# Two small helper products of a two-layer transformer kernel replaced: the relative distances' row written by GpSimd, the forget gate's partial sums added by ScalarE and VectorE

## The chip, the cores and the metric

The kernel runs on one core of a Trainium2 chip. The metric is the device time of one execution in microseconds (us), as the median of the runs shown. The core's engines are TensorE (PE in the profile, with its weight loads listed as PEld), VectorE (DVE), ScalarE (ACT), GpSimd (POOL) and SyncE (SP), which here only issues transfers. Each engine works through its own instructions in order and waits for the others by semaphores.

## The reference

A decoder trunk of two layers over 256 tokens with 1024 features, all in float32. Layer 0 mixes tokens by attention with a forget gate, layer 1 by attention with a learned bias on the relative distance (its block choice has no effect at this length, since 256 tokens are a single block). Each layer then has a feed-forward network (2816 wide) and a gated per-layer input.

```
for i in (0, 1):
    u = rmsnorm(h, attn_norm_g[i])
    if i == 0:                                   # forgetting attention, 16 heads of 64
        q, k, v, f_logit = split(u @ fox_w_in)   # f_logit: one column for each head
        log_f = log_sigmoid(f_logit + fox_b_f)
        c = cumsum(log_f over tokens)
        logits = q k^T / 8 + c[t] - c[s]         # causal
    else:                                        # relative bias from a table, 32 buckets x 16 heads
        q, k, v = split(u @ moba_w_in)
        logits = q k^T / 8 + rel_bias_table[bucket(t - s)]   # causal
    h += softmax(logits) v @ w_o[i]
    g, w = split(rmsnorm(h, ffn_norm_g[i]) @ ffn_w_in[i])
    h += (silu(g) * w) @ ffn_w_out[i]
    h += sigmoid(rmsnorm(h, ple_norm_g[i]) @ ple_w_gate[i]) * (p[i] @ ple_w_up[i])
return rmsnorm(h, final_norm_g)
```

`bucket` maps distances 0 to 15 to buckets of their own and larger ones to 16 buckets of growing width, the last of which holds everything from the 113th distance on.

## The kernel before, in words

The activations stay in SBUF for the whole run, features on partitions: `hx` holds 8 blocks of 128 features by 256 tokens. The weights are read once from DRAM as 216 tiles of 128 x 1024 numbers, in the order in which they are used, by SyncE's queue into a ring of six buffers (`raw`). Each is split in two for TensorE's faster float format: ScalarE copies it rounded into `whi`, VectorE subtracts that from `raw` into `wlo` (`half`, L188 and L189; `blocks` by way of L164 and L169). Each product is then three matmuls, high x high, high x low and low x high (`mm3`, L98 to L100), added in a PSUM bank. In what follows, tile k is the k-th weight tile.

The program is written as one sequence; a scheduler places the instructions on the engines' queues by its own estimate of when their inputs are ready, so that an edit moves neighbouring instructions too. `attention(0, ...)` begins with the value projection: for each of 8 feature blocks k it multiplies tokens by tile k into four banks `v` (the first three by L467, the others by `tokens`, L98 to L100). Between these stand a few helper steps:

- `nm.root()` and `nm.spread()` make the first norm's factors. The squares' sums `ss` are added over partitions by matmuls into `pr` (L250); VectorE turns them into the mean square `ms` (L251); GpSimd raises it to the power -0.5, `col` (L253); ScalarE and VectorE make the diagonal matrices `dg` from it, high and low part, two halves each (L257, L259); two matmuls by a matrix of ones spread them over all partitions into `pr` (L295), from where they are copied to `row`.
- `fox_bias` (called as `mid` in block k = 5) makes the forget gate. The gate's 16 weight columns `wf32`, padded to 32, are multiplied with `hx` in four column groups of TensorE at once (L376), so that the bank `pf` holds four partial sums on partitions 0, 32, 64 and 96. Before the change these are split into two parts (`fparts`) and added by a product with a 0/1 matrix `pick` (`total`, L386). `rest` then multiplies by the norm's row, adds the bias, takes the logarithm of the sigmoid, sums over tokens, and spreads the result through DRAM (`cd`) into `bias`, to which GpSimd adds the causal mask 32 times (L408, L409).
- `distances` makes `rv`, a row of 384 numbers for each head: the negated table entry of the bucket of each distance 255 to 0, and 1e30 beyond. Before the change it is a product of the table, split in two (`rr`), with a 0/1 matrix `ht` of buckets by distances (L425), and one VectorE instruction that negates it and adds the 1e30 from `rm` (L426). `moba_bias` stores it to DRAM (`d1`, L431, a transfer on SyncE's queue) and later spreads it for layer 1 (`d2`).

Small constants come in one transfer, `cs` from `cst` (L318): the identity, the causal mask, `pick`, the gate's weights, the table `rl` and the gate's bias. The matrix `hot` and the row `rm` have transfers of their own (L320, L322).

Of the kernel before, what the change touches and what calls it, by code (L numbers as in the profile page):

```python
# [15 lines left out]
P = 128  # L16
# [18 lines left out]
GN = 64  # L35
CST = 656
EARLY = 4
# [41 lines left out]
@with_exitstack  # L79
def trunk(ctx: ExitStack, tc: tile.TileContext, pt, w, cst, gf, hot, rvm, out):  # L80
    nc = tc.nc
# [6 lines left out]
    def bank(name):  # L88
        return ps.tile([P, 512], F32, tag="bank", name=name)

    def f32(ap):
        return ap.bitcast(F32)
# [32 lines left out]

    still0 = first_line[:, 16:17].unsqueeze(2)
    nc.gpsimd.memset(first_line[:, 16:17], 0.0)
    eps = first_line[:, 24:25]
# [8 lines left out]
    cs = one.tile([P, CST], F32, name="cs")  # L137
    ident, mask, pick32 = cs[:, 0:P], cs[:, P:2 * P], cs[:, 2 * P:3 * P]
    wf32 = cs[:, 3 * P:4 * P].rearrange("p (k h) -> p k h", h=H)
    rl, bfs = cs[0:BUCKETS, 4 * P:4 * P + H], cs[0:H, 4 * P + H:4 * P + H + 1]  # L140

# [176 lines left out]
    nc.sync.dma_start(cs, cst)  # L318
    hot32 = work.tile([BUCKETS, RVW], F32, tag="e", bufs=6, name="hot32")
    nc.sync.dma_start(hot32, hot)  # L320
    rm = work.tile([H, RVW], F32, tag="e", bufs=6, name="rm")
    nc.sync.dma_start(rm, rvm)  # L322
    ht = work.tile([P, RVW], F32R, tag="e", bufs=6, name="ht")
    nc.gpsimd.tensor_copy(ht, still0[:, 0].to_broadcast([P, RVW]))
    nc.gpsimd.tensor_copy(ht[0:BUCKETS], hot32)

    nhalf = tiny.tile([P, 2], F32, bufs=1, name="nhalf")
# [41 lines left out]
    def fox_bias(nm):  # L369
# [8 lines left out]

        pick = work.tile([P, P], F32R, tag="pt", bufs=6, name="pick")
        nc.gpsimd.tensor_copy(pick, pick32)  # L380
        parts = [work.tile([P, S], F32R, tag="pt", bufs=6, name=f"fparts{i}") for i in range(2)]
        split(*parts, pf[:, :S])

        def total():
            for i in range(2):
                mm(pf[:, S:2 * S], pick, parts[i], start=i == 0, stop=i == 1, skip_group_check=True)  # L386

        def rest():
            with tc.high_priority():
                f = work.tile([H, S], F32, tag="pt", bufs=6, name="f")  # L390
                nc.vector.tensor_tensor(f, pf[:H, S:2 * S], nm.row[:H, 1], op=ALU.mult)
                nc.vector.tensor_scalar(f, f, bfs, None, op0=ALU.add)
                a = work.tile([H, S], F32, tag="pt", bufs=6, name="fabs")
                nc.scalar.activation(a, f, AF.Abs)
                nc.scalar.activation(a, a, AF.Exp, scale=-1.0)
                nc.scalar.activation(a, a, AF.Ln, bias=1.0)
                nc.vector.scalar_tensor_tensor(f, f, 0.0, a, op0=ALU.min, op1=ALU.subtract)
                cum = work.tile([H, S], F32, tag="pt", bufs=6, name="cum")
                nc.vector.tensor_tensor_scan(cum, f, zero, 0.0, ALU.add, ALU.add)
                cd = dram.tile([H, S], F32, name="cd")  # L400
                nc.scalar.dma_start(cd, cum)
# [9 lines left out]

        return total, rest

    rv = work.tile([H, RVW], F32, tag="e", bufs=6, name="rv")

    rr = work.tile([P, 2, P], F32R, tag="pt", bufs=6, name="rr")
    nc.gpsimd.tensor_copy(rr, still0.to_broadcast([P, 2, P]))
    nc.gpsimd.tensor_copy(rr[0:BUCKETS, 0, 0:H], rl)
    nc.gpsimd.tensor_tensor(rr[0:BUCKETS, 1, 0:H], rl, f32(rr[0:BUCKETS, 0, 0:H]), op=ALU.subtract)

    def distances():

        pb = bank("pb")
        for i in range(2):
            mm(pb[:, :RVW], rr[:, i], ht, start=i == 0, stop=i == 1, skip_group_check=True)  # L425
        nc.vector.scalar_tensor_tensor(rv, pb[:H, :RVW], -1.0, rm, op0=ALU.mult, op1=ALU.add)  # L426

# [24 lines left out]
    def attention(layer, nm, mid, early, nf):  # L452
        vb = [bank(f"v{layer}_{b}") for b in range(4)]
        for c in range(4):
            wt = [early.pop(0) if early else half() for _ in range(2)]
            for kk in range(2):
# [12 lines left out]
                else:  # L469
                    for t, hf in units:  # L470
                        if layer == 0 and k == 5 and (t, hf) == units[0]:
                            total, rest = mid(nm)
                            nm.root()
                        if layer == 0 and k == 6 and (t, hf) == units[2]:
                            nm.spread(-0.125)
                            bias = rest()
                        cols = slice(hf * HC, (hf + 1) * HC)
                        tokens(vb[2 * t + hf], nm.k(k), t, (hi[:, cols], lo[:, cols]), k == 0, k == KT - 1)
# [3 lines left out]
                if layer == 0 and k == 5:  # L482
                    distances()
                    total()
            if layer == 1:
# [417 lines left out]
def _buckets():  # L903

    m = np.arange(RVW)
    n = np.maximum(S - 1 - m, 0)
    half = BUCKETS // 2
    nf = np.maximum(n, 1).astype(np.float32)
    large = half + (np.log(nf / np.float32(half)) / np.float32(math.log(MAX_DIST / half))
                    * np.float32(BUCKETS - half)).astype(np.int32)  # L910
    b = np.where(n < half, n, np.minimum(large, BUCKETS - 1))
    hot = np.zeros((BUCKETS, RVW), np.float32)
    hot[b[:S], m[:S]] = 1.0
    mask = np.zeros((H, RVW), np.float32)
    mask[:, S:] = BIG
    return hot, mask

# [66 lines left out]
```

## Time and profile before

| | us |
|---|---|
| median of 3 runs (lowest, highest) | 644.41 (643.93, 644.76) |
| span of the profiled execution | 642.4 |
| PE busy | 633.8 (99%) |
| DVE busy | 453.7 (71%) |
| ACT busy | 375.5 (58%) |
| POOL busy | 27.2 (4%) |

The profile is of one execution. Its span runs from the first to the last event on the core; no separate device time of that execution is recorded, so its own time is taken as the span plus the 2.0 us by which the median of the runs stands above it. The change lies in the first 30 us, where the page shows the transfers at 90% or more of their capacity and TensorE at its full granted clock. A row of a timeline gives the start, the duration (both us), the engine, the line, the operation, its output and inputs with their shapes, and in brackets how long the engine had been idle and what ended that. A row of the waits view gives who waited for whom, the sum in us, how often, and the longest.

### The profile page before, as it was taken

Reading aid. Unit: us, or ns where it says so; the run is one execution under the profiler, and the core shown is the slowest. Engines: PE = TensorE matmul, PEld = TensorE weight load, DVE = VectorE, ACT = ScalarE, POOL = GpSimd, SP = SyncE. Lnnn points to the kernel's source line nnn. Section 1 sums busy time; section 2 is a strip of 40 time slices with the busy share of each in tenths; the row PEclk is TensorE's granted clock in tenths of the full one; section 3 lists DMA queues with packets and bytes.
Section 4 is the critical chain, followed back from the end, with each engine's and each line's share of the span. In section 5 each row is a group of like instructions: output and inputs, shape, how many; then the busy total and the mean of one; then the engine's idle time right before and its main releaser. Section 6 shows DMA issues by size and latency. Waiting matters only on the chain.

```text
span 642.4 us, 13158 instructions
## 1 busy us (share of the span) xinstructions
PE 633.8 (99%) x5307; PEld 612.6 (95%) x5307; DVE 453.7 (71%) x781; ACT 375.5 (58%) x657; POOL 27.2 (4%) x55
## 2 busy tenths in 40 slices
PE   9999999999999999999999999999999999999995
PEld 7899999999999999999989999999999999999984
DVE  6877885786666666659896787578766666666665
ACT  8757675764444445458875586568444444454772
POOL 2118000000000000000000000000000000000002
PEclk9999999999999999999999999999999999999999
DMA  9779744376656566565687544335766666666501
GB/s 330 285 274 360 256 139 156 113 256 198 195 195 196 197 193 205 195 191 171 210 275 252 177 153 132 132 106 181 249 193 197 194 196 197 197 213 197 165 1 66
DMA packets 37020, 125.06 MB, mean 195 GB/s; under 512 B 3984, under 2 KB 6880, under 8 KB 36960
## 3 DMA queue, kind: packets, MB, share of 16 engines
q1 hardware_dynamic: 36640, 123.79, 58.3%
q8 instruction: 41, 0.67, 0.4%
q10 hardware_dynamic: 320, 0.44, 0.2%
q14 instruction: 19, 0.16, 0.1%
HBM read 123.13 MB, written 4.24 MB: 198 GB/s over the span
## 4 chain that ended last, share of the span: by engine, by line
PE 97%; DMA 1%; POOL 0%; issue 0%; ACT 0%; DVE 0%; POOLq 0%; DVEq 0%
PE gu L99 12%; PE gu L100 12%; PE gu L98 12%; PE fo L99 6%; PE fo L100 6%; PE fo L98 6%; PE pq L98 5%; PE pq L99 5%; PE pq L100 5%; PE wo L98 2%; PE wo L99 2%; PE wo L100 2%; PE pg L99 2%; PE pg L98 2%; PE pg L100 2%; PE v L98 2%
## 5 line engine op out<-in xcount | busy, mean ns | idle before, releaser
L189 DVE TENSOR_TENSOR wlo<-raw,whi 128x1024 fp32r<-128x1024 f32 (+1 forms) x198 | 237.6, 1205 | 110.5 <-ACT whi L188 105.1
L188 ACT ACTIVATE whi<-raw 128x1024 fp32r<-128x1024 f32 (+1 forms) x198 | 205.4, 1041 | 151.0 <-PE gu L99 56.3
L99 PE MATMUL gu<-g,whi 128*128 128x256 f32 x702 | 193.8, 276 | 0.0
L98 PE MATMUL gu<-g,whi 128*128 128x256 f32 x702 | 193.8, 276 | 0.0
L100 PE MATMUL gu<-g,wlo 128*128 128x256 f32 x702 | 193.8, 276 | 0.0
L100 PEld LDWEIGHTS gu<-g,wlo 128*128 128x128 f32 x702 | 131.8, 188 | 0.0
L98 PEld LDWEIGHTS gu<-g,whi 128*128 128x128 f32 x702 | 131.8, 188 | 0.0
L99 PEld LDWEIGHTS gu<-g,whi 128*128 128x128 f32 x702 | 131.8, 188 | 0.0
L98 PE MATMUL fo<-fh,whi 128*128 128x256 f32 x352 | 97.3, 276 | 0.0
L100 PE MATMUL fo<-fh,wlo 128*128 128x256 f32 x352 | 97.2, 276 | 0.0
L99 PE MATMUL fo<-fl,whi 128*128 128x256 f32 x352 | 97.2, 276 | 0.0
L98 PE MATMUL pq<-g,whi 128*128 128x256 f32 x256 | 71.1, 278 | 0.0
L100 PE MATMUL pq<-g,wlo 128*128 128x256 f32 x256 | 70.8, 276 | 0.0
L99 PE MATMUL pq<-g,whi 128*128 128x256 f32 x256 | 70.7, 276 | 0.0
L98 PEld LDWEIGHTS fo<-fh,whi 128*128 128x128 f32 x352 | 66.1, 188 | 0.0
L99 PEld LDWEIGHTS fo<-fl,whi 128*128 128x128 f32 x352 | 66.1, 188 | 0.0
L100 PEld LDWEIGHTS fo<-fh,wlo 128*128 128x128 f32 x352 | 66.1, 188 | 0.0
L98 PEld LDWEIGHTS pq<-g,whi 128*128 128x128 f32 x256 | 48.1, 188 | 1.1 <-issue 0.7
L99 PEld LDWEIGHTS pq<-g,whi 128*128 128x128 f32 x256 | 48.1, 188 | 0.1
L100 PEld LDWEIGHTS pq<-g,wlo 128*128 128x128 f32 x256 | 48.1, 188 | 0.0
L337 ACT ACTIVATE fh<-sg 128x256 fp32r<-128x256 f32 x44 | 18.1, 415 | 49.5 <-DVE sg L647 49.5
L164 ACT ACTIVATE whi<-raw 128x256 fp32r<-128x256 f32 (+3 forms) x44 | 25.5, 623 | 25.2 <-PE pq L99 8.3
(186 smaller groups left out, 983.9 us busy)
## 6 DMA issues: line engine op xcount, KB each, us to landing
raw<-w SPq DMA_DIRECT2D x212, 512.0 KB, 3.6
d<-d SPq DMA_DIRECT2D x4, 768.0 KB, 10.7
raw<-w SPq DMA_DIRECT2D x8, 256.0 KB, 4.4
bias<-d SPq DMA_DIRECT2D x4, 512.0 KB, 7.0
bias<-cd SPq DMA_DIRECT2D x2, 768.0 KB, 6.6
gx<-w SPq DMA_DIRECT2D x1, 512.0 KB, 5.3
bias<-cd SPq DMA_DIRECT2D x1, 512.0 KB, 4.3
p<-pt SPq DMA_DIRECT2D x2, 256.0 KB, 3.8
```

What stands on the lines that cost most here:

```text
L98: mm(o, ah, bh, start=start, stop=False, skip_group_check=True)
L99: mm(o, ah, bl, start=False, stop=False, skip_group_check=True)
L100: mm(o, al, bh, start=False, stop=stop, skip_group_check=True)
L164: nc.scalar.activation(o, raw[:, c], AF.Copy)
L188: nc.scalar.activation(hi[:, c], raw[:, c], AF.Copy)
L189: nc.vector.tensor_tensor(lo[:, c], raw[:, c], f32(hi[:, c]), op=ALU.subtract)
L337: nc.scalar.activation(hi, src, AF.Copy)
```

## The change

`distances` no longer multiplies. The table comes transposed and with its buckets in descending order in `cs` (`near`, one row for each head). GpSimd first fills `rv` with 1e30, early in the program. Distances of one bucket are neighbours in `rv`, so that the row falls into 32 runs, of 143, 14, 12, 10, 10, 8, 7, 6, 6, 5, 4, 4, 3, 3, 2, 3 and sixteen times 1 column; GpSimd writes each of the first 16 by one instruction that reads a single table column for all columns of the run and multiplies by -1, and the last 16 by one more. `fox_bias` no longer multiplies by `pick`: ScalarE copies the second, third and fourth partial sum out of PSUM onto partitions 0 to 15, and VectorE adds the first and the three copies. The operands `rr`, `ht`, `pick`, `hot` and `rm` with their GpSimd instructions and two transfers go, and `cst` shrinks from 656 to 448 columns.

```diff
-    ident, mask, pick32 = cs[:, 0:P], cs[:, P:2 * P], cs[:, 2 * P:3 * P]
-    wf32 = cs[:, 3 * P:4 * P].rearrange("p (k h) -> p k h", h=H)
-    rl, bfs = cs[0:BUCKETS, 4 * P:4 * P + H], cs[0:H, 4 * P + H:4 * P + H + 1]
+    ident, mask = cs[:, 0:P], cs[:, P:2 * P]
+    wf32 = cs[:, 2 * P:3 * P].rearrange("p (k h) -> p k h", h=H)
+    near, bfs = cs[0:H, 3 * P:3 * P + BUCKETS], cs[0:H, 3 * P + BUCKETS:3 * P + BUCKETS + 1]
...
     nc.sync.dma_start(cs, cst)
-    hot32 = work.tile([BUCKETS, RVW], F32, tag="e", bufs=6, name="hot32")
-    nc.sync.dma_start(hot32, hot)
-    rm = work.tile([H, RVW], F32, tag="e", bufs=6, name="rm")
-    nc.sync.dma_start(rm, rvm)
-    ht = work.tile([P, RVW], F32R, tag="e", bufs=6, name="ht")
-    nc.gpsimd.tensor_copy(ht, still0[:, 0].to_broadcast([P, RVW]))
-    nc.gpsimd.tensor_copy(ht[0:BUCKETS], hot32)
...
-        pick = work.tile([P, P], F32R, tag="pt", bufs=6, name="pick")
-        nc.gpsimd.tensor_copy(pick, pick32)
-        parts = [work.tile([P, S], F32R, tag="pt", bufs=6, name=f"fparts{i}") for i in range(2)]
-        split(*parts, pf[:, :S])
-
-        def total():
-            for i in range(2):
-                mm(pf[:, S:2 * S], pick, parts[i], start=i == 0, stop=i == 1, skip_group_check=True)
+        parts = [work.tile([H, S], F32, tag="pt", bufs=6, name=f"fparts{g}") for g in range(1, groups)]
+        for g in range(1, groups):
+            nc.scalar.activation(parts[g - 1], pf[GC * g:GC * g + H, :S], AF.Copy)
+        for g, q in enumerate(parts):
+            nc.vector.tensor_tensor(parts[0], pf[:H, :S] if g == 0 else parts[0], q, op=ALU.add)
...
-                nc.vector.tensor_tensor(f, pf[:H, S:2 * S], nm.row[:H, 1], op=ALU.mult)
+                nc.vector.tensor_tensor(f, parts[0], nm.row[:H, 1], op=ALU.mult)
...
-    rr = work.tile([P, 2, P], F32R, tag="pt", bufs=6, name="rr")
-    nc.gpsimd.tensor_copy(rr, still0.to_broadcast([P, 2, P]))
-    nc.gpsimd.tensor_copy(rr[0:BUCKETS, 0, 0:H], rl)
-    nc.gpsimd.tensor_tensor(rr[0:BUCKETS, 1, 0:H], rl, f32(rr[0:BUCKETS, 0, 0:H]), op=ALU.subtract)
+    nc.gpsimd.memset(rv, BIG)
 
     def distances():
 
-        pb = bank("pb")
-        for i in range(2):
-            mm(pb[:, :RVW], rr[:, i], ht, start=i == 0, stop=i == 1, skip_group_check=True)
-        nc.vector.scalar_tensor_tensor(rv, pb[:H, :RVW], -1.0, rm, op0=ALU.mult, op1=ALU.add)
+        runs = _runs()
+        one_each = sum(m1 - m0 == 1 for m0, m1 in runs)
+        for i, (m0, m1) in enumerate(runs[:len(runs) - one_each]):
+            nc.gpsimd.tensor_scalar(rv[:, m0:m1], near[:, i:i + 1].to_broadcast([H, m1 - m0]), -1.0, None, op0=ALU.mult)
+        nc.gpsimd.tensor_scalar(rv[:, S - one_each:S], near[:, BUCKETS - one_each:BUCKETS], -1.0, None, op0=ALU.mult)
...
                 if layer == 0 and k == 5:
                     distances()
-                    total()
...
+def _runs():
+
+    b = _buckets()
+    edges = [0] + [m for m in range(1, S) if b[m] != b[m - 1]] + [S]
+    assert len(edges) == BUCKETS + 1 and b[0] == BUCKETS - 1
+    return list(zip(edges, edges[1:]))
```

The edit also moves instructions in the engines' orders, at three places on which the prediction rests. A name's number tells buffers apart and differs between the two programs.

GpSimd, from the first instruction that needs `cs` to the root `col`. Before:

```order
L418 CAST rr<-cs 32x16
L380 CAST pick<-cs 128x128
L419 ISA
L419 TENSOR_TENSOR rr<-cs,rr 32x16
L325 CAST ht<-hot_153 32x384
L253 TENSOR_TENSOR col_277<-ms_273,nhalf 128x2
```

And now (the runs between the third and the last are left out):

```order
L410 ISA
L410 TENSOR_SCALAR rv<-cs 16x143
L410 TENSOR_SCALAR rv<-cs 16x14
...
L410 TENSOR_SCALAR rv<-cs 16x3
L411 TENSOR_SCALAR rv<-cs 16x16
L251 TENSOR_TENSOR col_269<-ms_265,nhalf 128x2
```

Four instructions between `cs` and `col` became seventeen.

VectorE, from the second sum of squares (`ss`) to the second half of `dg`. Before, `wlo` are the low parts of tiles 5, 6, 7 and the first quarter of tile 8:

```order
L234 TENSOR_TENSOR ss_225<-ss_225,sq_6_233 128x512
L236 TENSOR_TENSOR ss_225<-ss_225 128x256
L189 TENSOR_TENSOR wlo_239<-raw_237,whi_238 128x1024
L251 TENSOR_SCALAR ms_273<-pr_272 128x2
L189 TENSOR_TENSOR wlo_304<-raw_302,whi_303 128x1024
L338 TENSOR_TENSOR fparts_269<-pf,fparts_268 128x256
L189 TENSOR_TENSOR wlo_310<-raw_308,whi_309 128x1024
L169 TENSOR_TENSOR wlo_405<-raw_403,whi_404 128x256
L259 SCALAR_TENSOR_TENSOR dg_279<-cs,col_277,dg_279 128x128 x2
```

And now, the `wlo` being of tiles 5, 6 and 7:

```order
L232 TENSOR_TENSOR ss_214<-ss_214,sq_6_222 128x512
L187 TENSOR_TENSOR wlo_228<-raw_226,whi_227 128x1024
L234 TENSOR_TENSOR ss_214<-ss_214 128x256
L187 TENSOR_TENSOR wlo_307<-raw_305,whi_306 128x1024
L249 TENSOR_SCALAR ms_265<-pr_264 128x2
L373 TENSOR_TENSOR fparts_255<-pf,fparts_255 16x256
L373 TENSOR_TENSOR fparts_255<-fparts_255,fparts_256 16x256
L373 TENSOR_TENSOR fparts_255<-fparts_255,fparts_257 16x256
L257 SCALAR_TENSOR_TENSOR dg_271<-cs,col_269,dg_271 128x128
L187 TENSOR_TENSOR wlo_313<-raw_311,whi_312 128x1024
L257 SCALAR_TENSOR_TENSOR dg_271<-cs,col_269,dg_271 128x128
```

Tiles 5 and 6 moved ahead of the fold of `ss` and of `ms`, and tile 7 moved between the two halves of `dg`, which is now closer to the front.

SyncE's queue, from the constants on; `raw` are tiles 5 and up. Before:

```order
L318 DMA cs<-cst 128x656
L320 DMA hot_153<-hot 32x384
L322 DMA rm<-rvm 16x384
L185 DMA raw_237<-w 128x1024
L185 DMA raw_302<-w 128x1024
L185 DMA raw_308<-w 128x1024
L155 DMA raw_403<-w 128x1024
L185 DMA raw_435<-w 128x1024
L185 DMA raw_468<-w 128x1024
L185 DMA raw_498<-w 128x1024
L431 DMA d_391<-rv 16x384
```

And now:

```order
L316 DMA cs<-cst 128x448
L183 DMA raw_226<-w 128x1024
L183 DMA raw_305<-w 128x1024
L183 DMA raw_311<-w 128x1024
L416 DMA d_394<-rv 16x384
L153 DMA raw_406<-w 128x1024
```

The store of `rv` moved ahead of the loads of tiles 8 to 11.

More of the change, by code (lines that the diff above doesn't have):

```diff
@@ L35 @@
 GN = 64
-CST = 656
+CST = 448
 EARLY = 4
@@ L79, in trunk @@
 @with_exitstack
-def trunk(ctx: ExitStack, tc: tile.TileContext, pt, w, cst, gf, hot, rvm, out):
+def trunk(ctx: ExitStack, tc: tile.TileContext, pt, w, cst, gf, out):
     nc = tc.nc
@@ L124, in trunk @@
     table(AF.Square)
-    still0 = first_line[:, 16:17].unsqueeze(2)
-    nc.gpsimd.memset(first_line[:, 16:17], 0.0)
     eps = first_line[:, 24:25]
@@ L410, in rest @@
             return lambda i: (first[:, i], c[:, i])
-        return total, rest
+        return rest
     rv = work.tile([H, RVW], F32, tag="e", bufs=6, name="rv")
-    rr = work.tile([P, 2, P], F32R, tag="pt", bufs=6, name="rr")
-    nc.gpsimd.tensor_copy(rr, still0.to_broadcast([P, 2, P]))
-    nc.gpsimd.tensor_copy(rr[0:BUCKETS, 0, 0:H], rl)
-    nc.gpsimd.tensor_tensor(rr[0:BUCKETS, 1, 0:H], rl, f32(rr[0:BUCKETS, 0, 0:H]), op=ALU.subtract)
+    nc.gpsimd.memset(rv, BIG)
     def distances():
-        pb = bank("pb")
-        for i in range(2):
-            mm(pb[:, :RVW], rr[:, i], ht, start=i == 0, stop=i == 1, skip_group_check=True)
-        nc.vector.scalar_tensor_tensor(rv, pb[:H, :RVW], -1.0, rm, op0=ALU.mult, op1=ALU.add)
+        runs = _runs()
[3 more added lines that the diff above has]
+        nc.gpsimd.tensor_scalar(rv[:, S - one_each:S], near[:, BUCKETS - one_each:BUCKETS], -1.0, None, op0=ALU.mult)
     def moba_bias():
@@ L471, in attention @@
                         if layer == 0 and k == 5 and (t, hf) == units[0]:
-                            total, rest = mid(nm)
+                            rest = mid(nm)
                             nm.root()
@@ L903, in _buckets @@
 def _buckets():
-    m = np.arange(RVW)
-    n = np.maximum(S - 1 - m, 0)
+    n = S - 1 - np.arange(S)
     half = BUCKETS // 2
@@ L910, in _buckets @@
                     * np.float32(BUCKETS - half)).astype(np.int32)
[L911 to L916, printed above, removed]
+    return np.where(n < half, n, np.minimum(large, BUCKETS - 1))
+def _runs():
[3 more added lines that the diff above has]
+    return list(zip(edges, edges[1:]))
 def kernel(x, p, attn_norm_g, fox_w_in, fox_b_f, fox_w_o, moba_w_in, moba_w_o, rel_bias_table,
@@ L953 @@
     tri = np.where(np.arange(P)[None, :] > np.arange(P)[:, None], np.float32(BIG), np.float32(0))
-    hot, rvm = _buckets()
-    pick = (np.arange(P)[None, :] == np.arange(P)[:, None] % GC).astype(np.float32)
     cst = np.zeros((P, CST), np.float32)
-    cst[:, 0:P], cst[:, P:2 * P], cst[:, 2 * P:3 * P] = np.eye(P), tri, pick
-    cst[:, 3 * P:4 * P] = fw[:, 3 * D:].reshape(KT, P, H).transpose(1, 0, 2).reshape(P, -1)
-    cst[0:BUCKETS, 4 * P:4 * P + H], cst[0:H, 4 * P + H] = ar(rel_bias_table), ar(fox_b_f)[0]
+    cst[:, 0:P], cst[:, P:2 * P] = np.eye(P), tri
+    cst[:, 2 * P:3 * P] = fw[:, 3 * D:].reshape(KT, P, H).transpose(1, 0, 2).reshape(P, -1)
+    cst[0:H, 3 * P:3 * P + BUCKETS], cst[0:H, 3 * P + BUCKETS] = ar(rel_bias_table).T[:, ::-1], ar(fox_b_f)[0]
     xs = x[0].T.reshape(KT, P, S).transpose(1, 0, 2)
@@ L971 @@
         "gf": ar(final_norm_g)[None, :],
-        "hot": hot,
-        "rvm": rvm,
     }
```

## The prediction

> **What bounds the kernel now.** I read the page first, then the waits of TensorE (PE), then the chain of waits in order of time, and last the timelines of the other engines between 12 and 30 us. The page:
>
> ```profile
> span 642.4 us, 13158 instructions
> PE 633.8 (99%) x5307; PEld 612.6 (95%) x5307; DVE 453.7 (71%) x781; ACT 375.5 (58%) x657; POOL 27.2 (4%) x55
> ...
> PE 97%; DMA 1%; POOL 0%; issue 0%; ACT 0%; DVE 0%; POOLq 0%; DVEq 0%
> ```
>
> The reader is to see a program that is one long row of matmuls: PE makes 97% of the chain that ended last, GpSimd (POOL) almost nothing. The longest waits of PE and the only one of its matmuls show that nothing of size stands between them:
>
> ```profile
> PE cold L133 <- PEq L976: 0.8, 1, 0.8
> ...
> PEld v L467 <- ACT whi L188: 0.7, 1, 0.7
> ```
>
> So the time falls by what PE no longer does, and rises by every wait that the change puts in front of a matmul. The pieces of the chain that the change touches (start, us, what):
>
> ```profile
> 18.93 1.00 PE pf L376 x16
> ...
> 23.34 0.23 PE pf L386 x2
> ...
> 24.04 0.35 PE pb L425 x2
> ...
> 25.32 0.23 PE pr L295 x2
> ```
>
> L386 and L425 are the two helper products that go. L295 spreads the first norm's factors over the partitions from `dg`, and it keeps its place; it is where a wait can arise.
>
> **The products.** 0.23 + 0.35 us leave the chain, -0.58 us. No PE wait hides them, since PE has none there. All else that the change moves is off the chain in the kernel before, so its cost is what it makes PE wait.
>
> **The copies and adds for the forget gate.** The rows of the split and of 16x256 work of the same kind:
>
> ```profile
> 20.05 0.38 ACT L337 ACTIVATE fparts<-pf 128x256 fp32r<-128x256 f32 x1 [2.12 <-PE pf L376]
> 20.33 1.05 ACT L188 ACTIVATE whi<-raw 128x1024 fp32r<-128x1024 f32 x1
> ...
> 22.40 0.70 ACT L257 ACTIVATE dg<-cs,col 128x128 fp32r<-128x128 f32 x2 [0.72 <-POOL col L253]
> ...
> 30.70 0.40 ACT L394 ACTIVATE fabs<-f 16x256 f32<-16x256 f32 x1
> ```
>
> ```profile
> 20.50 0.16 DVE L251 TENSOR_SCALAR ms<-pr 128x2 f32<-128x2 f32 x1 [1.66 <-PE pr L250]
> 20.58 1.23 DVE L189 TENSOR_TENSOR wlo<-raw,whi 128x1024 fp32r<-128x1024 f32 x1
> 21.73 0.42 DVE L338 TENSOR_TENSOR fparts<-pf,fparts 128x256 fp32r<-128x256 f32 x1
> ...
> 23.53 0.61 DVE L259 SCALAR_TENSOR_TENSOR dg<-cs,col,dg 128x128 fp32r<-128x128 f32 x2
> ...
> 24.42 0.55 DVE L426 SCALAR_TENSOR_TENSOR rv<-pb,rm 16x384 f32<-16x384 f32 x1 [0.29 <-PE pb L425]
> ```
>
> ScalarE (ACT): three copies of 0.40 for one of 0.38, +0.8 us from 20.05. Behind them stands `whi` of weight tile 7 (the row of 20.33), which would end at about 22.2 and whose matmuls come after L295 in PE's order; `dg` waited for POOL until 22.40 anyhow. Hidden. VectorE (DVE): three adds of about 0.4 for 0.42 + 0.55, +0.25 us, in a stretch where it idled 1.66 us before 20.50; hidden too.
>
> **The transfers.** The constants shrink from 328 to 224 KB and two small loads go:
>
> ```profile
> 12.00:14.00 2.00, 2.00 (x10) 1.66 (x9) 2.00 (x5) 2.00 (x5) 0.00 (x0) 1.00 1.05 368
> ...
> cs<-cst SPq DMA_DIRECT2D x1, 328.0 KB, 6.2
> ```
>
> At 368 GB/s, 104 KB are 0.29 us: `cs` lands at about 13.8 instead of 14.09. PE does not wait for weights there, so nothing comes off the end.
>
> **The seventeen runs on GpSimd.** This is the real question. As the order in the section on the change shows, between the landing of `cs` and `col` (the first norm's root, which `dg` needs) GpSimd had four instructions. They become seventeen, and `col` stands behind all of them. Prices, from GpSimd's timeline:
>
> ```profile
> 14.09 0.31 POOL L418 CAST rr<-cs 32x16 fp32r<-32x16 f32 x1 [11.56 <-DMA cs<-cst]
> 14.35 0.28 POOL L380 CAST pick<-cs 128x128 fp32r<-128x128 f32 x1
> 14.69 1.10 POOL L419 TENSOR_TENSOR rr<-cs,rr 32x16 fp32r<-32x16 f32 x1
> ...
> 20.74 1.63 POOL L253 TENSOR_TENSOR col<-ms,nhalf 128x2 f32<-128x2 f32 x1 [4.04 <-DVE ms L251]
> ...
> 47.06 0.46 POOL L408 TENSOR_TENSOR bias<-bias,cs 128x128 f32<-128x128 f32 x1
> 47.48 1.45 POOL L409 TENSOR_TENSOR bias<-bias,cs 128x128 f32<-128x128 f32 x1
> ...
> 631.98 0.19 POOL L836 TENSOR_TENSOR colf<-ssf,msf 128x1 f32<-128x1 f32 x1 [11.94 <-ACT sqf L815]
> 632.25 0.55 POOL L846 TENSOR_TENSOR colf<-colf,nhalf 128x1 f32<-128x1 f32 x1
> 632.89 2.12 POOL L853 TENSOR_SCALAR end<-end,colf 128x512 f32<-128x512 f32 x1
> ```
>
> No row shows a TENSOR_SCALAR of 2 to 143 columns. Low end: 0.19 us (one column, nothing beside it), 17 x 0.19 = 3.2 us. Next: 0.26, from the start of the 32x16 copy to the next start, 4.4 us. High: the 512-column TENSOR_SCALAR, 2.12; as a price per column (4.1 ns x 256 columns) on top of 0.19 each it gives 4.3 us, as a fixed price it would be absurd beside 0.19. I take 0.19, the row nearest in size. Alone, the runs would thus end at 13.8 + 3.2 = 17.0 to 18.2 us, long before `col` may start at 20.74.
>
> They are not alone. Two of the rows above are far too long, 1.10 for 16 columns and 1.45 where its twin takes 0.46, and both end when a VectorE subtraction ends:
>
> ```profile
> 14.05 0.29 DVE L371 TENSOR_TENSOR fg<-cs,gx 128x128 f32<-128x128 f32 x1
> 14.31 1.40 DVE L189 TENSOR_TENSOR wlo<-raw,whi 128x1024 fp32r<-128x1024 f32 x1
> ...
> 47.07 1.54 DVE L189 TENSOR_TENSOR wlo<-raw,whi 128x1024 fp32r<-128x1024 f32 x1 [0.34 <-ACT whi L188]
> ```
>
> 14.31 + 1.40 = 15.71 against 14.69 + 1.10 = 15.79; 47.07 + 1.54 = 48.61 against 48.93. The subtraction too is longer than its usual 1.23, by about what GpSimd's earlier instruction still had to run (47.06 + 0.46 = 47.52). So each holds the other up for a whole instruction, and mostly they alternate. `col` itself is such a case: 1.63 beside the subtraction of 20.58 to 21.81, then 22.37 - 21.81 = 0.56, the 0.55 it takes undisturbed. [...]
>
> In VectorE's new order tile 6's subtraction precedes `ms` (the mean square that `col` needs), in what was idle time, but tile 7's stands between the two halves of `dg`. In strict alternation seven two-input instructions (`fg`, tile 4, two `ss` sums, tile 5, the `ss` fold, tile 6) run from 14.05 to about 20.6 and let eight runs through; nine are left, 9 x 0.19 = 1.7, and the runs end at 22.4. `col` ends 0.56 later, at 22.95. From there to L295: ACT's first half 0.40, `dg` 0.3, the subtraction 1.15 (20.58 to 21.73), `dg` 0.35, hand-overs 0.1: 2.3 us, 25.25. When PE gets there, and to two other places used below:
>
> ```profile
> 16.95 0.39 PE L99 MATMUL v<-wlo,g 128*128 128x512 f32 x1
> ...
> 25.15 0.39 PE L295 MATMUL pr<-dg,every 128*128 128x256 f32 x2
> ...
> 29.49 0.28 PE L98 MATMUL pq<-g,whi 128*128 128x256 f32 x1
> ```
>
> 25.15 - 0.58 = 24.57: PE waits 0.7 us. If two runs slip through per gap, the runs end by 21, `col` by 21.6, and PE waits nothing. I take the middle, +0.35 us, with 0 and (at 0.26 a run, ending at 23.2) 1.5 as ends.
>
> **The row's store in SyncE's queue.** Before, `d<-rv` stood behind the load of tile 11; now it stands behind tile 7, and tiles 8 to 11 wait for `rv`:
>
> ```profile
> 25.00 0.33 SPq L431 DMA_DIRECT2D d<-rv  x1
> 25.42 1.91 SPq L185 DMA_DIRECT2D raw<-w  x4
> ...
> raw<-w SPq DMA_DIRECT2D x212, 512.0 KB, 3.6
> ```
>
> With `rv` at 22.4, tile 8 is issued at 22.8, lands at 26.4 and is split by 27.5; its matmuls start at 29.49 - 0.58 = 28.9. It would bind from `rv` at 23.8 on, but by then L295 waits longer and pushes 28.9 out as far. Cost 0. Tile 12 goes out with it instead of at 25.42, so the loads catch up.
>
> **Sum.** -0.58 + 0.35 = -0.23 us. The span of the profiled execution, 642.4, becomes 642.2; the median of the runs stands 2.0 above that span, and I keep those 2.0: 644.41 - 0.23 = 644.2 us. A measurement of this kernel can tell about 0.2%, 1.3 us, from no change: 643.1 to 645.7.
>
> **Rivals.** *The runs lock VectorE out* (slower). GpSimd's copy of 14.35 ran to its end though the subtraction of 14.31 was queued: two in a row got through, so a row of short ones may keep the port. Then `fg` and tile 4's subtraction wait for all the runs, until 13.8 + 3.2 = 17.0 to 18.2, and the low part is ready 0.3 + 1.1 later, 18.4 to 19.6. PE wants it at 16.95 (tile 4's first L99), a wait of 1.5 to 2.7, net +0.9 to +2.1: 645.3 to 646.5. It decides from 0.21 us a run on. Against it: at 47.52 VectorE was let in though GpSimd's next had queued.
> *A run costs 0.4 us or more* (slower). Nine left make 3.6, the runs end at 24.2, PE waits 2.5, net +1.9: 646.3. Only the 2.12 row speaks for it.
> *GpSimd stands still before its first arithmetic instruction.* An ISA row stands ahead of the runs in the order. A hole of L us there would put the runs' end at 13.8 + L + 3.2, and the kernel would be slower than can be told from L = 6.6 on. Before, an ISA row stood ahead of L419 as well, where 0.06 us pass between 14.35 + 0.28 and 14.69, so I give it little. [...]
> *More than the products is won*, 643.0 or less. PE has no wait there to lose, and 0.58 is all it can shed; only an unseen effect, as of the later tiles' addresses, which move down by 832 bytes, could add to it.
>
> **Chances.** Forecast, with PE's wait between 0 and 1.5 us (643.8 to 645.4): 0.70. VectorE locked out: 0.14, two thirds of it beyond 645.7. Dear runs: 0.09. The hole: 0.02. More won: 0.05. Faster than 643.1: 0.05; slower than 645.7: 0.09 + 0.09 = 0.18, and 0.01 for a wait that I have not seen; the same: 0.76. The range, 643.4 to 646.4, leaves out the last rival below and the dearest ends above.
>
> **What the profile after would show.** Right: no L386 or L425 among PE's pieces; seventeen short TENSOR_SCALAR rows between 13.8 and 22.4, some stretched to over a microsecond beside `wlo`; `col` ending between 21.3 and 23.0; PE idle under 0.7 us before L293; the first `pq` matmul at 28.9 to 29.7. Wrong: PE idle before tile 4's low part near 17 us (lock-out); rows of 0.4 us with VectorE idle beside them; a hole ahead of the first run; or PE waiting for tile 8 near 29 us.

## The result: 651.1 us, 1.1% slower, and where the profile after puts it

The kernel after took 651.14 us (median of 4 runs, 650.67 to 651.69), the kernel before in the same comparison 644.32 (643.93 to 644.76): a ratio of 1.0106, 95% interval 1.0094 to 1.0118. The forecast was 644.2, with a range up to 646.4. The profiled execution took 650.67 us, so it can stand for the median; its own page reads:

```profile
span 648.9 us, 13157 instructions
...
PE 636.7 (98%) x5303; PEld 614.9 (95%) x5303; DVE 458.6 (71%) x782; ACT 376.0 (58%) x659; POOL 27.5 (4%) x66
```

PE has four matmuls less and is busy 2.9 us more, in a span that is 6.5 us longer: it both stood still and ran slower somewhere. The waits of PE name one place that the kernel before did not have, and a second behind it:

```profile
PE pq L98 <- DVE qkt L502: 3.3, 1, 3.3
PE sp L512 <- ACT pt L540: 0.9, 1, 0.9
```

**The part that the prediction looked at went as forecast.** GpSimd's timeline at the end of the runs, and PE's at the two places behind it:

```profile
21.38 0.26 POOL L411 TENSOR_SCALAR rv<-cs 16x16 f32<-16x16 f32 x1
21.61 0.72 POOL L251 TENSOR_TENSOR col<-ms,nhalf 128x2 f32<-128x2 f32 x1
```

```profile
24.54 0.45 PE L293 MATMUL pr<-dg,every 128*128 128x256 f32 x2
28.92 0.28 PE L98 MATMUL pq<-g,whi 128*128 128x256 f32 x1
```

The runs end at 21.6 and `col` at 22.3, PE reaches L293 at 24.54 without a wait, and `pq` begins at 28.92, 0.57 us earlier than the 29.49 of before. Up to here the two products are gained.

**The loss lies between 45 and 75 us.** VectorE's timeline there has one row that is unlike any other of its kind:

```profile
43.85 1.21 DVE L187 TENSOR_TENSOR wlo<-raw,whi 128x1024 fp32r<-128x1024 f32 x1
...
51.95 8.14 DVE L187 TENSOR_TENSOR wlo<-raw,whi 128x1024 fp32r<-128x1024 f32 x1 [5.79 <-ACT whi L186]
```

These are the low parts of tiles 18 and 19: the same work, 1.21 us and 8.14 us. GpSimd's timeline beside it, the 32 mask adds of L395 and L396 (first, sixteenth, seventeenth and last):

```profile
45.63 0.46 POOL L395 TENSOR_TENSOR bias<-bias,cs 128x128 f32<-128x128 f32 x1 [23.30 <-DMA bias<-cd]
...
51.88 0.46 POOL L396 TENSOR_TENSOR bias<-bias,cs 128x128 f32<-128x128 f32 x1
52.29 0.46 POOL L395 TENSOR_TENSOR bias<-bias,cs 128x128 f32<-128x128 f32 x1
...
58.55 0.47 POOL L396 TENSOR_TENSOR bias<-bias,cs 128x128 f32<-128x128 f32 x1
```

GpSimd loses nothing: one add every 0.42 us from first to last. The low part begins at 51.95, after 16 of them, and ends at 60.09, 1.07 us after the last add's end at 59.02, a little less than the 1.21 us that it takes alone. VectorE was shut out for all 16 adds that were left. In the kernel before the same subtraction, at 47.07, got in as soon as the add of 47.06 had ended. (In what follows, "the port" stands for whatever holds up an instruction of VectorE and one of GpSimd where they meet; the rows at 47.07 and 47.48 of before show such a meeting, 1.54 us for a subtraction that takes 1.21 alone and 1.45 us for an add that takes 0.46. What it is, the traces do not show.)

What hangs on it: tile 19's matmuls and `qkt` behind it on VectorE. PE's timeline:

```profile
58.44 0.28 PE L100 MATMUL pq<-g,wlo 128*128 128x256 f32 x1
62.04 0.37 PE L98 MATMUL pq<-g,whi 128*128 128x256 f32 x1 [3.33 <-DVE qkt L502]
```

And the stretches around it (start and end, length, then busy time and instructions of PE, weight loads, DVE, ACT, POOL, then the granted clock, the DMA share and GB/s):

```profile
60.00:62.00 2.00, 0.00 (x0) 0.00 (x0) 2.00 (x5) 0.00 (x0) 0.00 (x0) 1.00 0.28 70
62.00:64.00 2.00, 1.96 (x10) 1.99 (x11) 2.00 (x9) 1.86 (x8) 0.00 (x0) 0.56 0.83 268
64.00:66.00 2.00, 2.00 (x12) 2.00 (x12) 2.00 (x13) 0.75 (x4) 0.00 (x0) 0.59 0.81 209
66.00:68.00 2.00, 2.00 (x20) 2.00 (x19) 1.97 (x14) 2.00 (x10) 0.00 (x0) 1.00 0.91 333
```

After the 3.33 us of standstill PE gets 0.56 and 0.59 of its clock for 4 us and does 22 matmuls where it would do 40. That is 4 x (1 - 0.575) = 1.7 us. The wait for `pt` behind it costs more than its 0.9 us. The 16 matmuls `sp`, up to the first `po`, in the kernel before and then after:

```profile
66.63 1.58 PE L528 MATMUL sp<-qkt 64*128 64x128 f32 x16
68.14 2.17 PE L567 MATMUL po<-pt,vf 128*64 128x256 f32 x24
```

```profile
71.25 1.17 PE L512 MATMUL sp<-qkt 64*128 64x128 f32 x8
73.30 1.29 PE L512 MATMUL sp<-qkt 64*128 64x128 f32 x8 [0.89 <-ACT pt L540]
74.52 2.17 PE L551 MATMUL po<-pt,vf 128*64 128x256 f32 x24
```

They take 1.51 us before and 3.27 after, 1.76 more. Up to 58 us the matmuls start 0.57 us earlier than the same ones of before, at 74.52 `po` starts 6.38 later: 6.95 of the 7.1 us that lie between the 0.6 gained early and the 6.5 lost at the end arise here. (3.33, 1.7 and 1.76 make 6.8 of them.)

**Why the subtraction came so late.** In SyncE's queue the three `bias<-cd` loads (2 MB) stood behind tile 19 before and stand ahead of it now. The order of the two programs, between tiles 18 and 20, `-` before and `+` after, numbers left out:

```
 DMA raw18<-w 128x1024
-DMA raw19<-w 128x1024
 DMA bias0<-cd 128x1024
 DMA bias0<-cd 128x1536 x2
+DMA raw19<-w 128x1024
 DMA raw20<-w 128x1024
```

ScalarE's timelines show what it did to tile 19's high part, first before, then after:

```profile
45.98 1.07 ACT L188 ACTIVATE whi<-raw 128x1024 fp32r<-128x1024 f32 x1 [1.70 <-PE pq L99]
```

```profile
50.86 1.06 ACT L186 ACTIVATE whi<-raw 128x1024 fp32r<-128x1024 f32 x1 [7.16 <-PE pq L99]
```

It comes 4.9 us later. (The profile names PE as the releaser; DMA runs at 406 GB/s and a share of 1.01 from 46 to 50 us in the stretch view, moving the loads that went ahead.) So in the kernel after VectorE had no subtraction of this kind from 45.06 to 51.95 us, while GpSimd added and added.

That left a question that decides what to do about it: is it the late tile, the seventeen runs, or the length of GpSimd's undisturbed stream that shuts VectorE out?

### The profile page after: what moved, and what is told of

Its sections match the earlier page's. It is cut to its first block, busy times and chain, and to the rows that moved or that the text cites. A ratio compares the mean times of both kernels' runs of the same rounds, so it can differ in the third digit from the quotient of the medians.

```text
span 648.9 us, 13157 instructions
## 1 busy us (share of the span) xinstructions
PE 636.7 (98%) x5303; PEld 614.9 (95%) x5303; DVE 458.6 (71%) x782; ACT 376.0 (58%) x659; POOL 27.5 (4%) x66
## 4 chain that ended last, share of the span: by engine, by line
PE 95%; issue 2%; ACT 1%; DMA 1%; DVE 1%; POOL 0%; POOLq 0%; DVEq 0%; ACTq 0%
PE gu L98 12%; PE gu L99 12%; PE gu L100 12%; PE fo L98 6%; PE fo L99 6%; PE fo L100 6%; PE pq L98 4%; PE pq L99 4%; PE pq L100 4%; PE wo L98 2%; PE wo L99 2%; PE wo L100 2%; PE pg L98 2%; PE pg L100 2%; PE pg L99 2%; PE v L98 2%
## 5 line engine op out<-in xcount | busy, mean ns | idle before, releaser
L187 DVE TENSOR_TENSOR wlo<-raw,whi 128x1024 fp32r<-128x1024 f32 (+1 forms) x198 | 243.8, 1236 | 114.4 <-ACT whi L186 108.8
L98 PE MATMUL pq<-g,whi 128*128 128x256 f32 x256 | 72.0, 281 | 3.3 <-DVE qkt L502 3.3
L99 PE MATMUL pq<-g,whi 128*128 128x256 f32 x256 | 71.5, 279 | 0.0
L98 PEld LDWEIGHTS pq<-g,whi 128*128 128x128 f32 x256 | 48.8, 191 | 4.6 <-issue 4.2
L99 PEld LDWEIGHTS pq<-g,whi 128*128 128x128 f32 x256 | 48.8, 191 | 0.1
```

What stands on the lines that cost most here:

```text
L98: mm(o, ah, bh, start=start, stop=False, skip_group_check=True)
L99: mm(o, ah, bl, start=False, stop=False, skip_group_check=True)
L187: nc.vector.tensor_tensor(lo[:, c], raw[:, c], f32(hi[:, c]), op=ALU.subtract)
```

## Experiments

Four theories are named in the expectations. A: the late tile does it. B: the seventeen small GpSimd instructions on 16 partitions do it, so that VectorE is no longer let in at the mask adds, whenever tile 19 comes. C: chance. D, formed after the first seven runs: what counts is how many adds have run since the two engines last met on the port.

### Each half of the suspected cause by itself

**t19_first** is the kernel after with tile 19's load queued ahead of the three loads (`spreads`); the lines that collect `loads` and `spreads` are left out here:

```diff
+    def load_made(i):
+        if i == 19:
+            for d in spreads.values():
+                tc.add_manual_dep(d.ins, loads[i].ins.name, mybir.DependencyInfo(
+                    mybir.DependencyClass.NoSync, mybir.DependencyReason.DATA), reason="tile 19 first")
```

> The kernel after, with one load moved in SyncE's queue and nothing else: tile 19's weight load is issued ahead of the three bias<-cd loads, as in the kernel before, and no longer behind them. Theory A (tile 19 comes late behind the three loads, VectorE has nothing to do from 45 to 52 us, GpSimd's mask adds run on uninterrupted and then shut VectorE out until the last of them): tile 19's low part is again among the adds from their start and takes under 1.6 us instead of 8.14, TensorE does not stop at 58 us, and the time is 643.5 to 644.0, 0.6 us under the kernel before (the two products of 0.23 and 0.35 us are gone). [...]

By B a VectorE instruction of over 5 us would still be there, and the time would stay at 650 to 652.

Measured: 645.55 us, ratio 1.0039 (1.0011 to 1.0066); seven of ten executions took 644.8 to 645.7, the others 647.6, 651.6 and 652.1. VectorE in the profiled execution (645.69 us):

```profile
47.13 1.23 DVE L195 TENSOR_TENSOR wlo<-raw,whi 128x1024 fp32r<-128x1024 f32 x1 [0.34 <-ACT whi L194]
53.28 1.80 DVE L174 TENSOR_TENSOR wlo<-raw,whi 128x256 fp32r<-128x256 f32 x2 [4.93 <-ACT whi L169]
```

Tile 19 is cured, as A said, but the loads now come late, VectorE idles 4.93 us before tile 20 instead, and three of ten executions still lose some microseconds. Both theories missed the time.

**t19_last** is the kernel before with the one move that A blames, tile 19 behind the loads.

> The kernel before, both products kept, with tile 19's weight load issued behind the three bias<-cd loads, as it stands in the kernel after (the stores of d2 and two of VectorE's later splits also come a little earlier in their queues). Theory A: tile 19's low part comes only after some 6 us of mask adds, is shut out by the rest of them (6 to 9 us in place of 1.5), TensorE waits some 3 us near 60 us and then runs at a lower granted clock; the time is 650 to 652 without either part of the change. Theory B: the low part is let in after one add as before, at most 1.6 us, and the time stays within 1 us of 644.3.

Measured: 644.30 us, ratio 1.0014 (0.9995 to 1.0032): eight executions at 644.1 to 645.1, two at 648.3 and 648.6.

```profile
51.49 1.34 DVE L197 TENSOR_TENSOR wlo<-raw,whi 128x1024 fp32r<-128x1024 f32 x1 [4.70 <-ACT whi L196]
```

As late as in the kernel after, and let in. A in its plain form falls. (The two at 648 us have no trace. Their mean granted clock, 0.998 and 0.997, is that of the eight others, 0.996 to 0.998, while the profiled executions with a long low part have 0.991 to 0.995; whether they were locked stays open.)

**gate_only** and **dist_only** make one half of the change each. In both, the scheduler also puts tile 19 behind the loads.

> The kernel before with the gate's half of the change alone: ScalarE copies three quarters, VectorE adds them, the pick product of 0.23 us is gone; the distances' row still comes from TensorE's product, and no run is written by GpSimd. In SyncE's queue of this kernel tile 19's load also stands behind the three bias<-cd loads. Theory A: 650 to 652, with the long low part of tile 19. Theory B: no runs, so no lock: 644.0 to 644.3. If a third cause in the gate's part makes the time (the copies delay ScalarE's halves of tiles 13 to 15): slow here too, but without an instruction of VectorE of over 5 us near 52 us.

> The kernel before with the distances' half of the change alone: GpSimd writes the row in 17 small instructions, the product of 0.35 us with its preparation is gone; the gate's pick product stays. In SyncE's queue tile 19's load also stands behind the three bias<-cd loads. Theory A: 650 to 652, with the long low part of tile 19. Theory B: 650 to 652 as well. Were the gate's part the cause: 644.0 or less.

Measured: gate_only 644.39 us, ratio 1.0013 (0.9993 to 1.0033), with two of ten executions at 648.8 and 648.9; dist_only 652.38 us, ratio 1.0124 (1.0109 to 1.0139), all four between 651.7 and 652.9. Tile 19's low part, first gate_only, then dist_only:

```profile
50.13 1.57 DVE L189 TENSOR_TENSOR wlo<-raw,whi 128x1024 fp32r<-128x1024 f32 x1 [3.13 <-ACT whi L188]
```

```profile
53.15 8.26 DVE L188 TENSOR_TENSOR wlo<-raw,whi 128x1024 fp32r<-128x1024 f32 x1 [5.44 <-ACT whi L187]
```

The distances' half alone makes the whole loss, the gate's half none in eight executions of ten (the other two, again at a clock of 0.998 and 0.997, stay open). At this point B looked right.

### Are the runs themselves to blame?

**t19_last_runs** adds to t19_last seventeen small GpSimd writes that are overwritten afterwards:

```diff
+        at = 0
+        for i, n in enumerate(RUNS):
+            nc.gpsimd.tensor_scalar(rv[:, at:at + n], cs[0:H, i:i + 1].to_broadcast([H, n]), -1.0, None, op0=ALU.mult)
+            at += n
         pb = bank("pb")
```

> The kernel of the run t19_last (the kernel before with tile 19's load behind the three bias<-cd loads) plus 17 GpSimd instructions that write runs of 143 to 3 columns on 16 partitions of rv, ahead of L253's col as in the kernel after; the product overwrites them, so they do nothing for the result, and no other row of any engine's order differs. [...] Theory C (each execution draws anew whether VectorE is let in after some 15 adds, runs or not): as t19_last, a median near 644.3 with one or two executions in ten at 648.5.

By B tile 19's low part would take over 5 us in nearly every execution, with a median of 648 to 652.

Measured: 650.25 us, ratio 1.0079 (1.0059 to 1.0100); one of ten executions at 645.0, nine from 647.5 to 651.4.

```profile
55.59 8.10 DVE L198 TENSOR_TENSOR wlo<-raw,whi 128x1024 fp32r<-128x1024 f32 x1 [9.08 <-ACT whi L197]
```

**runs_all** is the kernel after with the runs on all 128 partitions, so that no small instruction on 16 partitions is left and every other row of the engines' orders is that of the kernel after (`near`, the runs and the store follow `rv`; those lines are left out here):

```diff
-    rv = work.tile([H, RVW], F32, tag="e", bufs=6, name="rv")
+    rv = work.tile([P, RVW], F32, tag="e", bufs=6, name="rv")
```

> [...] Theory A, sharpened (a stream that starts on a free port and runs 15 adds undisturbed locks VectorE out): still 650 to 652, with the low part of 8 us. [...]

By B the low part would be let in after one or two adds (under 1.6 us), with a median of 643.5 to 644.5, although tile 19 still comes late; by C some executions would be fast and some slow.

Measured: 647.41 us, ratio 1.0044 (1.0030 to 1.0059); five executions, 645.1, 646.0, 647.4, 647.8 and 648.0. The profiled one is the fastest of them, and there the low part is let in:

```profile
52.17 1.34 DVE L187 TENSOR_TENSOR wlo<-raw,whi 128x1024 fp32r<-128x1024 f32 x1 [5.30 <-ACT whi L186]
```

The first result fits B; the second is what C gave, with a median between those of B and A. Each of the two kernels differs from the one it starts from in one more thing, though. In t19_last_runs the runs delay `col`, with it `cum` (scanned at 38.52 us instead of 36.42) and the loads; the stream begins at 49.28 on a free port, and 16 adds run before the low part comes. In t19_last the first add, at 45.18, still met tile 18's low part, and 14 ran from there. In runs_all it was 14 again.

**port_trials** asks the port alone, without any of the kernel around it.

> No part of the reference is computed here. 36 trials one after the other: 26 GpSimd adds of 128x128 back to back, as the mask adds are; a VectorE subtraction of 128x1024, as a low part is, that comes after 1, 3 or 6 ScalarE copies of 128x1024 (some 4, 9 or 16 adds); the stream's start on a free port, or 0.3 us (B) or 0.9 us (T) into another such subtraction; and ahead of some trials 17 small GpSimd writes on 16 partitions or on 128. [...] Theory A, sharpened: it waits in the trials with a free start and 6 copies, whatever writes there were, and not in those with one copy or a blocked start. Theory C: long and short ones in each kind.

By B the subtraction would be let in ahead of the first writes on 16 partitions and behind writes on 128, and would wait for the last add behind writes on 16.

Measured, by the rows of the 36 trials: the subtraction that came after 1, 3 or 8 adds was let in within 1.33 us, 8 times of 8. After 16 adds from a free start it waited for the last one (5.4 us) 14 times of 14, and the first two of these stood ahead of any write on 16 partitions:

```profile
30.08 5.37 DVE L73 TENSOR_TENSOR wlo<-raw,whi 128x1024 fp32r<-128x1024 f32 x1 [17.35 <-ACT whi L72]
...
86.60 5.36 DVE L73 TENSOR_TENSOR wlo<-raw,whi 128x1024 fp32r<-128x1024 f32 x1 [8.19 <-ACT whi L72]
```

After a start beside another subtraction, with 16 adds begun in the one kind and 14 in the other, it waited 10 times of 14. There the first add met the other subtraction, so that 15 and 13 had run since the meeting: let in 1 time of 6 and 3 times of 8. B falls: the runs are not needed for the lock, nor do writes on 128 partitions prevent it (2 of 2 locked from a free start). What separates long from short is the number of adds, with a stretch, here at 13 and 15, in which either happens.

### How many adds shut the port

**port_curve** varies that number, and how the adds are cut.

> No part of the reference is computed here. 40 trials: 32 GpSimd adds of 128x128 back to back from a free port; a VectorE subtraction of 128x1024 comes after 1, 2, 3, 4, 5, 6 or 8 ScalarE copies of about 1.03 us (some 3, 6, 8, 11, 13, 16, 21 adds in); 26 trials so, then 7 with the same work in 16 adds of 128x256, then 7 with single adds of which the ninth has to wait some 0.2 us for ScalarE. Theory D (what decides is how many adds have run since GpSimd and VectorE last met on the port or GpSimd last waited): always let in (under 1.7 us) with up to 3 copies, nearly never with 6 and 8, a mixture at 4 and 5; with the pause after the eighth add, let in at 4 and 6 copies as well; with adds twice as wide, let in at 4 copies and likely at 6, since only half as many have run. Theory C (chance, whatever the number): short and long ones at each number alike.

From the rows, ScalarE copies ahead, adds begun, and how often the subtraction was let in within 1.7 us:

| adds of 128x128, undisturbed | 3 | 6 | 8 | 11 | 14 | 16 | 21 or 22 |
|---|---|---|---|---|---|---|---|
| copies | 1 | 2 | 3 | 4 | 5 | 6 | 8 |
| let in | 2 of 2 | 3 of 3 | 4 of 4 | 5 of 5 | 3 of 5 | 0 of 5 | 0 of 2 |

With one wait of GpSimd after the eighth add: 7 of 7 let in. The three of them that tell something came after 16, 16 and 22 adds in all, that is 8, 8 and 14 since the wait. With adds of 128x256: let in after 5, 7 and 10 adds, 6 of 6, the last of these 6.48 us after the stream's start; locked after 13 (one trial). So in these trials it is the number of instructions without a meeting or a wait that counts rather than the time: 6.48 us of single adds are 16, and 0 of 5 were let in there, against 2 of 2 after ten wide ones. Rows of VectorE's timeline: 16 adds, 11, 14 (locked), 14 (let in), ten wide ones, 16 with the wait:

```profile
17.93 7.81 DVE L65 TENSOR_TENSOR wlo<-raw,whi 128x1024 fp32r<-128x1024 f32 x1 [9.18 <-ACT whi L64]
...
49.51 1.35 DVE L65 TENSOR_TENSOR wlo<-raw,whi 128x1024 fp32r<-128x1024 f32 x1 [18.70 <-ACT whi L64]
...
117.92 8.90 DVE L65 TENSOR_TENSOR wlo<-raw,whi 128x1024 fp32r<-128x1024 f32 x1 [17.74 <-ACT whi L64]
...
185.44 1.50 DVE L65 TENSOR_TENSOR wlo<-raw,whi 128x1024 fp32r<-128x1024 f32 x1 [18.56 <-ACT whi L64]
...
470.57 1.48 DVE L65 TENSOR_TENSOR wlo<-raw,whi 128x1024 fp32r<-128x1024 f32 x1 [16.46 <-ACT whi L64]
...
574.89 1.22 DVE L65 TENSOR_TENSOR wlo<-raw,whi 128x1024 fp32r<-128x1024 f32 x1 [18.48 <-ACT whi L64]
```

With this the profiled executions of all the kernels fall into line. Adds begun since the last meeting (or since the stream's free start) when the next low part came, counted in GpSimd's timelines:

| kernel | before | in_turn (below) | gate_only | t19_first | t19_last | runs_all | dist_only | after | t19_last_runs |
|---|---|---|---|---|---|---|---|---|---|
| adds | 4 | 5 | 9 | 12 | 14 | 14 | 14 | 16 | 16 |
| low part, us | 1.54 | 1.49 | 1.57 | 0.67 (256 columns) | 1.34 | 1.34 | 8.26 | 8.14 | 8.10 |

Up to 12 all are let in, at 14 either happens, at 16 none. If executions of one kernel vary by an add or so, that would make the spread of t19_first and runs_all; only one execution of each has a trace, so that last step is argued. It would not make gate_only's two executions of 648.8 and 648.9 us, since its trace has 9.

**no_mask** takes the stream away, and with it the causal mask of the first layer, and leaves tile 19 late:

```diff
-            for i in range(H):
-                nc.gpsimd.tensor_tensor(first[:, i], c[:, i, 0:P], mask, op=ALU.add)
-                nc.gpsimd.tensor_tensor(c[:, i, P:S], c[:, i, P:S], mask, op=ALU.add)
-            return lambda i: (first[:, i], c[:, i])
+            nc.gpsimd.tensor_copy(first[:, 0, 0:1], c[:, 0, 0:1])
+            return lambda i: (c[:, i, 0:P], c[:, i])
```

> The kernel after without the 32 mask adds (GpSimd writes one column instead): the causal mask of the first layer is left out, and the order of no other engine changes. Tile 19 still comes late behind the three loads. Theories A and D: without a stream there is nothing to lock VectorE out, tile 19's low part takes 1.2 us, TensorE does not stop at 58 us, and the time is 643.4 to 644.0, 0.6 us below the kernel before. If the late tile itself, not the lock, costs the time: 646 or more.

Measured: 643.88 us, ratio 0.9996 (0.9988 to 1.0005); 0.36 us below the kernel before, not to be told from no change. The late low part is short, also in the profiled execution, the slowest of the ten (645.68 us):

```profile
53.80 1.22 DVE L187 TENSOR_TENSOR wlo<-raw,whi 128x1024 fp32r<-128x1024 f32 x1 [5.67 <-ACT whi L186]
```

The late tile costs nothing that can be measured by itself. Lock and stream together cost some 7 us (6.8 above the kernel before in the one, 0.4 below it in the other).

**in_turn** mends the cause where it arose, in SyncE's queue: bias, tile 19, bias, tile 20, bias. `ahead(a, b)` queues the load `a` ahead of `b`; `spreads` are the three loads by their first head.

```diff
+        if i == 19:
+            ahead(spreads[0], loads[19])
+            ahead(loads[19], spreads[4])
+        if i == 20:
+            ahead(spreads[4], loads[20])
+            ahead(loads[20], spreads[10])
```

> The kernel after with SyncE's queue in the order bias, tile 19, bias, tile 20, bias instead of the three bias<-cd loads in a row; no other row of any engine's order differs. VectorE's low parts of tiles 19 and 20 then come 1.5 to 4 us earlier, within some 8 adds of the last meeting, and GpSimd's later adds wait for their loads. Theory D: no low part over 2 us, 643.5 to 644.5. Theory B: locked as before, 650 to 652.

Measured: 644.90 us, ratio 1.0008 (0.9999 to 1.0016), twelve executions from 643.9 to 646.6, none near 650; the median is 0.4 above the range that theory D gave. VectorE's row, and PE's at the spread, from the slowest of the twelve:

```profile
49.41 1.49 DVE L202 TENSOR_TENSOR wlo<-raw,whi 128x1024 fp32r<-128x1024 f32 x1 [1.41 <-ACT whi L201]
```

```profile
25.47 0.39 PE L308 MATMUL pr<-dg,every 128*128 128x256 f32 x1 [0.82 <-DVE dg L272]
```

The lock is gone with every run in its old place, which is against B once more. The second row is the wait that the prediction was about: in this execution the runs ended at 22.5 us, `col` at 23.2, and PE waited 0.82.

**wide_adds** halves the number of adds: `first[:, h0:h1]` and `c[:, h0:h1, P:S]` for two heads at a time.

> The kernel after with the mask added for two heads in one instruction, 16 GpSimd adds of 128x256 in place of 32 of 128x128; same loads, same order on every other engine. Tile 19's low part then comes after 7 or 8 adds instead of 15. Theory D, if the number of instructions counts: it is let in after one add, under 2.3 us, and the time is 643.6 to 644.6. If the time of the uninterrupted stream counts rather than the number of adds: still locked until the stream's end, 650 to 652.

Measured: 650.56 us, ratio 1.0106 (1.0091 to 1.0122); four executions, 648.3, 650.0, 651.2, 652.8. Theory D missed the time here, and the median lies in the range that was expected if the time of the stream counted and not the number. In the profiled execution, the fastest, D holds for the subtraction, which came after 8 wide adds (9 with the first, which met tile 18's low part):

```profile
52.59 1.57 DVE L187 TENSOR_TENSOR wlo<-raw,whi 128x1024 fp32r<-128x1024 f32 x1 [5.04 <-ACT whi L186]
```

What costs there is another place, four microseconds of granted clock at a mean of 0.60 after a wait of PE for `pt` of 0.9 us (start and end first, the clock third from the end):

```profile
70.00:74.00 4.00, 4.00 (x28) 2.55 (x28) 3.37 (x20) 4.00 (x18) 0.00 (x0) 0.60 0.97 275
```

Whether the three slower executions were locked stays open; they have no trace. So this kernel does not decide between number and time; the trials of port_curve do, with few trials.

**tuned** is in_turn with the runs and their store moved into the first layer's feed-forward part, where nothing waits for them; ScalarE first writes the negated table (`turned`), from which the runs copy.

> The kernel of the run in_turn, with the 17 runs and their store moved from 14 to 22 us into the first layer's feed-forward part (behind ScalarE's SiLU of its fourth block), where GpSimd has nothing else to do and the row is not yet wanted. The queue order bias, tile 19, bias, tile 20, bias stays. Expected from the rows of in_turn and no_mask: col is no longer behind the runs (22.5 us in in_turn), so TensorE's wait of 0.8 us for dg at L308 goes, cum, cd and the mask adds come about 1 us earlier, and no low part takes over 2 us: 643.4 to 644.1, that is 0.2 to 0.8 us below the kernel before. If the runs beside the feed-forward part cost VectorE time that TensorE waits for: 644.5 or more. If the 0.9 us wait of TensorE for pt near 70 us stays as well: 644.0 to 644.6.

Measured: 644.10 us, ratio 0.9996 (0.9987 to 1.0005). In the profiled execution VectorE's row of tile 19 is 1.53 us and PE waits neither for `dg` nor for `pt`; GpSimd writes the runs at 138 us:

```profile
138.27 6.99 POOL L426 TENSOR_SCALAR rv<-turned 16x143 f32<-16x143 f32 x16 [39.19 <-ACT turned L420]
```

So the change can be had without its loss, and then it is worth no more than this kernel's measurement can tell from nothing: none of the versions beats the kernel before.

## Why the prediction was wrong

**Right: the products.** -0.58 us; `pq` began 0.57 us earlier, and L386 and L425 are gone.

**Right: the runs' price and their alternation with VectorE.** Unblocked runs took 0.21 to 0.26 us at a pitch of 0.20 (forecast 0.19), the stretched ones 1.15 beside `wlo`; they ended at 21.6 and `col` at 22.3 (forecast 22.4 and 22.95, with `col` between 21.3 and 23.0). No hole stood ahead of the first run, at 13.92 us.

**Right in kind: PE's wait at the spread.** Forecast 0.35 us between 0 and 1.5: none in the profiled execution after, 0.82 in in_turn's, 0.8 in no_mask's, 0.6 in wide_adds'. Whether the forecast's whole sum of -0.23 us was right cannot be told: without the lock the kernel stands 0.36 us below the kernel before in no_mask, 0.1 below it in tuned and 0.66 above it in in_turn, and none of these is clear of no change.

**Right: the store of `rv` ahead of tiles 8 to 11 cost nothing.** PE waits for none of these tiles. (The transfers are not at 90% of their capacity all through the first 30 us, as the part on the time before has it: in the kernel before the stretch view gives a share of 0.11 from 22 to 24 us and 0.04 from 24 to 26.)

**Wrong: "All else that the change moves is off the chain in the kernel before, so its cost is what it makes PE wait".** The sentence is true, but the working behind it stops at 30 us. The order of SyncE's queue was shown down to tile 8; eleven weight tiles further it moves tile 19 behind 2 MB of other loads. So a fourth place moved besides the three that the part on the change shows, and the sum put it at nothing without asking what it triggers. It cost 6.8 us against the kernel before. PE did not wait for tile 19's load as such, as no_mask shows; its lateness took away the meetings of VectorE with GpSimd that had kept the port open, and the low part took 8.14 us instead of 1.54.

**Wrong: "So each holds the other up for a whole instruction, and mostly they alternate".** The rows it rests on, 47.06 to 47.52, show a VectorE instruction that comes after four adds. From there to the rule that a VectorE instruction gets in after one of GpSimd's, however many have run, was a step that no row carried. The runs of 16 and 14 adds show that it fails for a longer stream: shut out for 16 further instructions in the kernel after. After four adds the trace of before shows a subtraction held up by one add at most (1.54 us at 47.07); after sixteen, that of the kernel after shows one held up by a queue of adds for 6.7 us more (52.29 to 59.02).

**The rival had the mechanism and the wrong place.** "The runs lock VectorE out" was looked for near 17 us, beside tile 4, where runs and VectorE's instructions in fact met seven times between 14 and 20 us (seven runs of 0.36 to 1.17 us, against 0.21 to 0.26 undisturbed). The 32 mask adds, twice as many and back to back, stood in the same trace and were read at one meeting only.

## What to carry to other kernels

When a change moves loads in a queue, follow each moved load to the engine that splits or uses it, also where nothing waited for it before: it may have been what broke up another engine's stream. In these traces VectorE and GpSimd alternate only while they keep meeting (one subtraction took 1.54 us after 4 adds and 8.14 after 16); a dozen or more back-to-back GpSimd adds (in port_curve the subtraction was let in 5 times of 5 after 11, 3 of 5 after 14 and 0 of 5 after 16) should get a wait in their middle (tried in port_curve alone), or loads dealt out so that the two engines meet (in_turn and tuned). Read the whole difference in order that a small edit makes, not its neighbourhood alone, before the sum is called complete.

## What the runs showed of the hardware

A back-to-back stream of GpSimd adds of 128x128 lets a VectorE subtraction of 128x1024 in as soon as the add then running ends if up to 11 have run undisturbed (14 of 14 trials of port_curve), sometimes at 14 (3 of 5), and not at all from 16 on (0 of 7, and 0 of 14 in port_trials) until the stream ends. There is nothing between: in all 76 trials the subtraction got in after at most one further add, or behind the last. A wait of GpSimd sets the count back (3 of 3 let in after 16 to 22 adds in all). Why the number of adds decides, no trace shows.

PE's granted clock fell after a standstill of 3.33 us: to 0.50 from 62.5 to 65.5 us, which makes the 0.56 and 0.59 of the two stretches, and added 1.7 us to it. In wide_adds it fell to a mean of 0.60 from 70 to 74 us after a wait of only 0.9 us, and in in_turn and in the kernel after it stayed at 1.00 after the same 0.9 us; that difference stays open.
